# A hand-ordered list of operations for a row-wise sum of reciprocals is replaced by another list

## The chip, the cores and the metric

The kernel runs on one core of one Trainium2 chip. The metric is device time in microseconds (us), the median over several executions. One more execution was recorded by the hardware profiler; every time of an instruction comes from that one.

## The reference

```python
"x": np.abs(np.random.randn(32, 512, 1024)).astype(np.float32) + 1e-6

def reference(x):
    return np.sum(1.0 / x, axis=-1).astype(np.float32)
```

The input holds 32 x 512 = 16,384 vectors of 1024 fp32 values, 67.1 MB. The output is one sum for each vector.

## The kernel before

The vectors are laid over 128 partitions, 128 vectors for each. What the kernel calls a row r is one vector in every partition: a tile of 128 x 1024 fp32, 512 KB. The rows lie in a ring of 40 places in SBUF (`ring`, row r in place r % 40).

The kernel does not divide element by element. It splits a row into its halves a and b and uses 1/a + 1/b = (a + b) / (ab). So half as many reciprocals are needed, and these are made by ScalarE as exp(-ln(ab)), with a scale of 2^17 that is taken out again in the last step. The steps of a row are:

- **D** (line 185, SP queue): the load. `D10` loads the next ten rows with one DMA.
- **P** (line 197, POOL), or **W** (line 218, DVE), or **C** and **V**: the product ab into a slot of `prod`. C (line 207) lets PE copy the half b into a PSUM bank by a matmul with the identity, V (line 218) multiplies on DVE with that bank; W multiplies two SBUF operands on DVE.
- **L** (line 240, ACT): Ln of the product, in place.
- **E** (line 249, ACT): Exp of minus that. With a bank number (`E8+2@6`) the result goes to PSUM, without one it stays in `prod`.
- **S** (line 230, PE): a + b into a PSUM bank, by two matmuls with the identity. Only some rows have it.
- **R** (line 265, DVE): the sum over the row. A row with S multiplies the 512 reciprocals with the 512 sums in PSUM and accumulates. A row without S multiplies all 1024 elements in the ring with the reciprocals, used twice, and accumulates; that instruction has twice the columns.

The order of all this is written out by hand in the string `PLAN`. A token is the step's letter, the row, `+2` where two neighbouring rows share an instruction, and after `@` a PSUM bank or, for L, the first of 22 slots of `prod`. Each engine executes its own tokens strictly in the order of the list; POOL, ACT, DVE, PE and the SP queue run beside each other and wait for one another through semaphores that follow from who reads and writes which ring place, slot or bank. So a token that has to wait holds up everything behind it on its engine.

The last two rows, 126 and 127, are cut in two halves of columns. The pieces are numbered 126 and 127 (the first halves) and 128 and 129 (the second halves), have 256-column instructions where others have 512, and are loaded one by one (256 KB each):

```python
def place(r):
    if r < LAST:
        return r, 0, H
    part, q = divmod(r - LAST, F - LAST)
    return LAST + q, part * H, H // 2
```

Loads use a DMA each, split where the ring wraps. A place in the ring may be written again when its row's product and its S (or, without S, its R) are done, so a D token stands behind those steps of the row 40 places earlier. After the last token one DMA writes the sums (line 282).

Of the kernel before, what the change touches and what calls it, by code (L numbers as in the profile page):

```python
# [11 lines left out]
def kernel(  # L12
# [22 lines left out]


    PLAN = """
        D2 D10 D15 D13 P0+2 C3@3 S2@0 V3 P2 L0@0 L1@1 C11@3 S3@1 E0@6 E1@7 P4+2 V11 L2@3 L3@2
        R0 S6@2 E2 E3 R1 P6+2 L4+2@4 R2 R3 E4+2@6 S7@0 P8+2 L6+2@8 R4 S10@1 E6+2 R5 D7 P10
        L8+2@10 R6 R7 S11@2 E8+2@6 L10+2@6 R8 E10+2 R9 R10 R11 P12+2 C19@3 S14@0 V19 P14+2  # L40
        L12+2@12 S15@1 E12+2@6 S18@2 R12 P16+2 L14+2@16 R13 E14+2 R14 P18 L16+2@18 R15 S19@0
        E16+2@6 P20+2 L18+2@14 R16 D10 S22@1 E18+2 R17 P22+2 L20+2@20 R18 R19 E20+2@6 S23@2
        P24+2 L22+2@0 R20 S26@0 E22+2 R21 D7 P26 L24+2@2 R22 C27@3 R23 E24+2@6 P28+2 S27@1
        V27 R24 L26+2@4 C35@3 R25 E26+2 P30+2 S30@2 L28+2@8 V35 R26 E28+2@6 R27 S31@0 P32+2
        L30+2@10 R28 E30+2 S34@1 R29 D8 P34 L32+2@12 R30 R31 P36+2 E32+2@6 S35@2 L34+2@6 R32
        C43@3 E34+2 R33 P38+2 S38@0 L36+2@16 R34 R35 E36+2@6 S39@1 V43 P40+2 L38+2@18 R36
        S42@2 E38+2 R37 D8 P42 L40+2@20 R38 R39 E40+2@6 S43@0 P44+2 L42+2@14 R40 S46@1 E42+2
        R41 D4 L44+2@0 R42 R43 E44+2@6 P46+2 C51@3 R44 S47@0 V51 P48+2 L46+2@2 R45 S50@2
        E46+2 R46 P50 L48+2@8 R47 S51@1 E48+2@6 P52+2 L50+2@4 R48 S54@0 E50+2 R49 D6 P54+2
        C59@3 L52+2@10 R50 R51 E52+2@6 S55@2 V59 P56+2 L54+2@12 R52 S58@1 E54+2 R53 D6 P58  # L50
        L56+2@16 R54 R55 S59@0 E56+2@6 P60+2 L58+2@6 R56 S62@2 E58+2 R57 D4 P62+2 L60+2@18
        R58 R59 C67@3 E60+2@6 P64+2 S63@0 L62+2@20 V67 R60 E62+2 S66@1 R61 D4 P66 L64+2@14
        R62 E64+2@6 P68+2 R63 S67@2 L66+2@0 R64 E66+2 S70@0 R65 D3 P70+2 L68+2@2 R66 R67
        E68+2@6 S71@1 L70+2@8 R68 D2 P72+2 C75@3 E70+2 R69 D3 S74@2 V75 P74 L72+2@4 R70 R71
        S75@0 E72+2@6 P76+2 L74+2@10 R72 S78@1 E74+2 R73 D2 D1 P78+2 L76+2@12 C83@6 R74 R75
        E76+2@4 S79@2 V83 P81 L78+2@16 R76 D2 S81@0 L83@6 W80 E78+2 W82 E83@7 R77 D2 D1
        S80@3 D1 D1 L82@7 L80+2@18 R83 P86 S86@4 E82@6 R78 P87 L86@20 R79 E80+2 S84@1 R82 D1
        D1 P84 D1 E86 R80 P89 L84@21 S89@2 R81 E84 R86 P85 L89@0 R84 E89 W88 L85@1 R89 E85@7
        P90+2 C93@6 L87+2@14 R85 D1 C95@5 E87+2@3 V93 S92@0 V95 P94 L90+2@2 R88 L95@4 S93@1
        P92 R87 D2 D1 D1 E90+2@6 E95@5 P98 R91 S97@2 L92+2@8 P99 R90 L94@5 S96@3 E92+2 R95  # L60
        P96+2 E94@7 L98+2@10 R92 R94 E98+2@5 P101+2 S100@0 R93 L96+2@12 R98 E96+2 R99 P100
        L101+2@6 R97 L100@16 P106 C104@7 R96 E101+2@5 S105@1 V104 P105 E100 R102 L104@19
        P107 S104@2 L105+2@17 R101 E104 P108 R100 E105+2 S106@3 R104 L107+2@20 W103 R105
        L103@0 P109 C110@7 R106 E107+2@5 S111@0 V110 P111 E103@4 R107 L109@1 P113 S112@1
        L110+2@14 R108 E109@7 P114 R103 E110+2 S110@2 W112 L113+2@2 R111 L112@4 P115 S116@3
        R109 E113+2@5 R110 P116 L115@5 R114 E112 E115@7 C118@4 P117 L116@10 R112 S117@0 V118
        E116 P119 L117@11 R115 L118@8 P120 S119@1 E117 R116 E118@7 R117 P121 L119+2@12 R118
        S120@0 E119+2 P122 R113 L121@9 R119 P123 L122@6 R120 E121@7 E122@6 R121 P124 S124@0
        L123@7 E123@5 R122 P125 L124@16 S125@1 E124 R123 P127 L125@19 L127@17 W126 S126@2
        E125 W128 P129 R124 L126@18 S129@3 E127@7 R125 E126 S128@0 L129@21 R127 L128@20 E129  # L70
        R126 E128 R129 R128
    """.split()

    Ln = mybir.ActivationFunctionType.Ln
# [238 lines left out]
```

## Time and profile before

| what | value |
|---|---|
| median of 4 runs | 169.12 us (169.03 to 169.23) |
| the profiled execution | 169.04 us |
| its span, first to last instruction | 167.2 us |
| busy PE, DVE, ACT, POOL | 132.7, 128.3, 133.0, 128.0 us |
| bytes read | 67.11 MB, 402 GB/s over the span |
| loads | 32, from 7,680 KB down to 256 KB |

Busy time counts compute instructions; waits, semaphores and the issue of DMAs do not count. The profile's page cuts the span into 40 slices and gives the busy share of each in tenths. The view of stretches gives busy microseconds of each engine in a stretch of time, with the number of instructions in brackets. The chain of waits is followed back from the last instruction, at each step to what released it. In a timeline a row has the start, the time, the engine, the line, the operation with its tiles and shapes, and how many instructions were merged; what stands in square brackets is idle time before it.

### The profile page before, as it was taken

To read this page: it belongs to the slowest core of one execution; us is meant where nothing else is said; L and a number is where in the kernel's file an instruction comes from. 1 tells how busy PE (TensorE), PEld (TensorE's weight loads), DVE (VectorE), ACT (ScalarE), POOL (GpSimd) and SP (SyncE) were. 2 spreads that over 40 slices of the span, in tenths; PEclk is the share of its full clock that TensorE was granted. 3 is DMA by queue.
4 is the path that set the end of the run, shared out by engine and by line. 5 is a ranking of instruction groups with operands and counts; after the bars stand their busy time and mean duration, and the time that the engine had idled before them with its cause. 6 is when DMAs were issued, how large, how long until landed. Compare 5 with 4: busy or idle time off the path is not lost.

```text
span 167.2 us, 1334 instructions
## 1 busy us (share of the span) xinstructions
PE 132.7 (79%) x292; PEld 54.9 (33%) x292; DVE 128.3 (77%) x283; ACT 133.0 (80%) x161; POOL 128.0 (77%) x80
## 2 busy tenths in 40 slices
PE   0000799949989999977998999999699679989692
PEld 0000333214433434323333434434244134424261
DVE  0000129864789989886798898799999999999994
ACT  3040255917999999977999997999899999999992
POOL 1500795049999999939999997966899997979970
PEclk9999999987999999999999999999999999999998
DMA  5999999999999998999999999999999999999910
GB/s 186 535 392 392 470 470 470 470 408 408 408 408 407 432 472 367 451 423 412 423 463 416 439 404 449 423 437 412 419 427 424 425 427 411 418 408 411 397 63 16
DMA packets 4760, 67.26 MB, mean 402 GB/s; under 512 B 528, under 2 KB 656, under 8 KB 2192
## 3 DMA queue, kind: packets, MB, share of 16 engines
q1 hardware_dynamic: 4752, 67.18, 94.9%
q14 instruction: 6, 0.05, 0.1%
q8 instruction: 2, 0.03, 0.1%
HBM read 67.11 MB, written 0.07 MB: 402 GB/s over the span
## 4 chain that ended last, share of the span: by engine, by line
DMA 61%; POOL 14%; DVE 10%; issue 9%; ACT 3%; PE 1%; SPq 0%; DVEq 0%; POOLq 0%
DMA ring<-in_x_dram 61%; POOL prod L197 14%; DVE ring L265 6%; DVE prod L265 3%; ACT prod L240 1%; ACT ps L249 1%; DVE prod L218 1%; PE ps L207 1%; DVE sums L265 0%; SPq L185 0%; DVEq L308 0%; POOLq L197 0%
## 5 line engine op out<-in xcount | busy, mean ns | idle before, releaser
L197 POOL TENSOR_TENSOR prod<-ring 128x1024 f32<-128x1024 f32 (+2 forms) x74 | 127.3, 1754 | 33.7 <-DMA ring<-in_x_dram 31.7
L230 PE MATMUL ps<-ring,ident 128*128 128x512 f32 (+1 forms) x260 | 118.0, 601 | 5.5 <-DVE sums L265 4.2
L240 ACT ACTIVATE prod<-prod 128x1024 f32<-128x1024 f32 (+2 forms) x80 | 69.1, 876 | 24.9 <-POOL prod L197 23.2
L265 DVE CUSTOM_DVE_ANT_1 ring<-ring,ps 128x1024 f32<-128x1024 f32 (+1 forms) x65 | 76.3, 1208 | 9.0 <-ACT ps L249 9.0
L230 PEld LDWEIGHTS ps<-ring,ident 128*128 128x128 f32 x260 | 49.2, 194 | 72.9 <-issue 50.2
L265 DVE CUSTOM_DVE_ANT_0 prod<-prod,ps 128x512 f32<-128x512 f32 (+1 forms) x63 | 40.7, 678 | 1.3 <-ACT prod L249 1.3
L207 PE MATMUL ps<-ring,ident 128*128 128x512 f32 x32 | 18.3, 658 | 25.8 <-DMA ring<-in_x_dram 25.8
L249 ACT ACTIVATE ps<-prod 128x1024 f32<-128x1024 f32 (+2 forms) x40 | 33.9, 854 | 4.7 <-DVE sums L265 3.9
L249 ACT ACTIVATE prod<-prod 128x1024 f32<-128x1024 f32 (+2 forms) x40 | 34.6, 875 | 0.8
L218 DVE TENSOR_TENSOR prod<-ring,ps 128x512 f32<-128x512 f32 x16 | 10.9, 684 | 26.1 <-PE ps L207 25.8
L207 PEld LDWEIGHTS ps<-ring,ident 128*128 128x128 f32 x32 | 5.7, 201 | 35.8 <-issue 21.1
L265 DVE DVE_READ_ACCUMULATOR2_ANT sums<- 128x1 f32 x130 | 10.7, 82 | 0.0
L218 DVE TENSOR_TENSOR prod<-ring 128x512 f32<-128x512 f32 (+1 forms) x7 | 4.5, 661 | 0.0
L83 ACT ACT_TABLE_LOAD x1 | 1.3, 1283 | 0.7 <-PEq L297 0.7
L265 DVE CUSTOM_DVE_ANT_0 prod<-prod,ps,sums 128x256 f32<-128x256 f32 x2 | 0.9, 474 | 0.0
masks.py:197 POOL MEMSET ident<- 128x128 f32 x1 | 0.2, 205 | 0.3 <-POOLq L297 0.3
masks.py:199 POOL TENSOR_SCALAR_AFFINE_SELECT ident<-ident 128x128 f32<-128x128 f32 x1 | 0.3, 292 | 0.1
L297 POOL MEMSET const-float32-0.0<- 128x1 f32 x1 | 0.1, 98 | 0.2 <-issue 0.2
L297 POOL MEMSET const-bfloat16-1.0<- 128x1 bf16 x1 | 0.1, 101 | 0.0
L297 POOL MEMSET const-uint8-127<- 128x1 uint8 x1 | 0.1, 101 | 0.0
L297 POOL MEMSET const-float32-1.0<- 128x1 f32 x1 | 0.1, 98 | 0.0
## 6 DMA issues: line engine op xcount, KB each, us to landing
ring<-in_x_dram SPq DMA_DIRECT2D x2, 5120.0 KB, 21.9
ring<-in_x_dram SPq DMA_DIRECT2D x2, 4096.0 KB, 32.4
ring<-in_x_dram SPq DMA_DIRECT2D x1, 7680.0 KB, 34.2
ring<-in_x_dram SPq DMA_DIRECT2D x2, 3584.0 KB, 30.3
ring<-in_x_dram SPq DMA_DIRECT2D x1, 6656.0 KB, 49.5
ring<-in_x_dram SPq DMA_DIRECT2D x3, 2048.0 KB, 34.8
ring<-in_x_dram SPq DMA_DIRECT2D x2, 3072.0 KB, 32.5
ring<-in_x_dram SPq DMA_DIRECT2D x5, 1024.0 KB, 26.0
```

Source lines behind the costliest of these rows:

```text
L83: nc.scalar.add_instruction(mybir.InstLoadActFuncSet(name=nc.get_next_instruction_name(), act_func_set_id=act_sets.index("natural_log_exp_ ...
L197: inst = nc.gpsimd.tensor_tensor(out=prod[:, p : p + m, :w], in0=ring[:, a : a + m, at : at + w], in1=ring[:, a : a + m, at + w : at + 2 * w],
L207: inst = nc.tensor.matmul(ps[:, b, : place(r)[2]], lhsT=ident, rhs=xs(r, 1), start=True, stop=True,)
L218: inst = nc.vector.tensor_tensor(out=prod[:, p, :w], in0=xs(r, 0), in1=in1, op=mult)
L230: inst = nc.tensor.matmul(ps[:, b, : place(r)[2]], lhsT=ident, rhs=xs(r, h), start=h == 0, stop=h == 1,)
L240: inst = nc.scalar.activation(out=pg, in_=pg, func=Ln, scale=S)
L249: inst = nc.scalar.activation(out=rc, in_=pg, func=Exp, scale=-1.0)
L265: inst = nc.vector.tensor_tensor_reduce(out=row, in0=row, in1=other, scale=S, scalar=total if q in summed else 0.0, op0=mult, op1=add, acc ...
L297: nc = _bacc.Bacc("TRN2", target_bir_lowering=False, num_devices=1)
```

## The change

Only the string `PLAN` changes. The tokens for each row stay of the same kinds; their order, the sizes of the loads, the pairing of rows, the slots and banks change. Up to row 79 the same rows have P, C and V, and S as before. From row 80 on the choice which row is multiplied by which engine, and which row has an S, is another: P is done for rows 83, 82, 85, 84, 86, 91, ... instead of 81, 86, 87, 84, 89, 85, ..., and the four half-row pieces get their product from P (before: 126 and 128 from W, 127 and 129 from P).

The loads were 2, 10, 15, 13, 7, 10, 7, 8, 8, 4, 6, 6, 4, 4, 3, 2, 3, 2, 1, 2, 2 rows, then 7 single rows and 4 half-rows, 32 in all. They become 2, 10, 14, 14, 10, 10, 6, 8, 6, 6, 6, 4, 4, 3, 3, 3, 2, 2, 2 rows, then 11 single rows and 4 half-rows, 34 in all.

The new list, the old one being in the code above:

```diff
     PLAN = """
+        D2 D10 D14 D14 P0+2 C3@3 S2@0 V3 P2 L0+2@0 C11@3 S3@1 E0+2@6 P4+2 V11 L2+2@2 R0 S6@2
+        E2+2 R1 P6+2 L4+2@4 R2 R3 E4+2@6 S7@0 P8+2 L6+2@8 R4 S10@1 E6+2 R5 P10 L8+2@10 R6 R7
+        S11@2 E8+2@6 L10+2@6 R8 E10+2 R9 D10 R10 R11 P12+2 C19@3 S14@0 V19 P14+2 L12+2@12
+        S15@1 E12+2@6 S18@2 R12 P16+2 L14+2@16 R13 E14+2 R14 P18 L16+2@18 R15 S19@0 E16+2@6
+        P20+2 L18+2@14 R16 S22@1 E18+2 R17 D10 P22+2 L20+2@20 R18 R19 E20+2@6 S23@2 P24+2
+        L22+2@0 R20 E22+2 R21 L24+2@2 R22 R23 E24+2@6 P26 C27@3 R24 S26@0 P28+2 V27 R25 D6
+        L26+2@4 C35@3 E26+2 S27@1 P30+2 V35 L28+2@8 R26 S30@2 R27 E28+2@6 P32+2 L30+2@10 R28
+        S31@0 E30+2 R29 P34 L32+2@12 S34@1 R30 R31 E32+2@6 P36+2 S35@0 L34+2@6 R32 E34+2 R33
+        D8 P38+2 S38@2 L36+2@16 R34 R35 E36+2@6 C43@3 P40+2 L38+2@18 S39@0 R36 E38+2 V43
+        S42@1 R37 D6 P42 L40+2@14 R38 E40+2@6 P44+2 R39 S43@2 L42+2@20 R40 E42+2 R41 S46@0
+        P46+2 L44+2@0 R42 R43 E44+2@6 S47@1 P48+2 L46+2@2 R44 E46+2 R45 D6 L48+2@4 P50 C51@3
+        R46 R47 S50@0 E48+2@6 V51 P52+2 R48 L50+2@8 C59@3 E50+2 R49 S51@1 D6 P54+2 L52+2@10
+        V59 R50 E52+2@6 S54@2 R51 P56+2 L54+2@12 R52 S55@0 E54+2 R53 D4 P58 L56+2@16 R54
+        S58@1 R55 E56+2@6 P60+2 S59@0 L58+2@6 R56 E58+2 R57 D4 P62+2 S62@2 L60+2@14 R58 R59
+        E60+2@6 S63@1 P64+2 L62+2@18 R60 E62+2 R61 D3 L64+2@20 R62 P66 C67@3 R63 E64+2@6
+        S66@0 V67 P68+2 R64 L66+2@0 S67@1 E66+2 R65 D3 P70+2 L68+2@2 R66 S70@2 R67 E68+2@6
+        P72+2 S71@0 L70+2@4 R68 D3 E70+2 R69 D2 C75@3 P74 L72+2@10 R70 S74@1 V75 E72+2@6
+        P76+2 R71 S75@2 L74+2@8 R72 D2 E74+2 R73 D2 D1 P78+2 S78@0 L76+2@12 R74 R75 E76+2@6
+        S79@1 L78+2@16 R76 D1 P83 C81@5 E78+2 R77 D1 D1 D1 P82 S83@2 L83@6 V81 P85 E83 R78
+        L82@7 S80@3 R79 L81@14 P84 R83 E82 E81@7 W80 D1 S82@0 L85@15 R81 D1 D1 D1 L84@18
+        E85@6 E84@5 R85 P86 C88@7 L80@19 E80 R82 C87@4 P91 L86@20 R80 S91@0 E86@6 V88 P89+2
+        L91@21 V87 L88@0 R86 S88@1 E91 E88 R91 L87@3 P95 R84 D1 D1 D1 S92@2 L89+2@1 P94 R88
+        E87@7 E89+2@5 S93@0 R87 D1 D1 D1 P93 L94+2@4 R90 P92 L93@10 R89 E94+2@3 C98@7 P96
+        E93 R95 S97@1 L92@11 P99 L96@8 R94 E92 S96@4 E96 W97 L99@9 V98 L97@12 P100+2 R92
+        E99@7 S102@3 R96 E97 R99 L98@13 E98@6 P102 R97 L100+2@16 R98 P103 C105@7 L102@6
+        E100+2@4 R93 S105@1 P104 V105 E102 R101 L103@14 S103@0 L104@15 R102 E103 P106 E104@7
+        R100 C107@6 R103 P108 L105+2@18 S106@2 V107 E105+2 R104 P109+2 S109@0 L107+2@20 R106
+        R105 E107+2@6 S110@2 P111 L109+2@0 R107 P112 E109+2 R108 C114@6 P113 L111+2@2 R110
+        S113@1 R109 E111+2@4 P115 V114 L113@7 R111 P116 S116@0 L114+2@4 R112 E113 P117
+        E114+2@6 S117@2 R113 P118 L116+2@8 R115 E116+2 P119 S119@1 R114 L118@11 R117 P120
+        L119@13 R116 E118@7 E119 R118 P121 S121@0 L120@12 E120@6 R119 P122 L121@10 S122@2
+        R120 E121 P123 L122@16 R121 E122 S123@1 W124 L123@17 R122 L124@6 E123 W125 S125@0
+        E124@7 R123 P126 L125@15 R124 P127 L126@14 E125 S128@1 P128 E126@6 R125 L127@18 P129
+        S129@2 L128@19 R126 E127@7 E128 R127 L129@20 R128 E129 R129
     """.split()
```

More of the change, by code (lines that the diff above doesn't have):

```diff
@@ L37 @@
     PLAN = """
[L38 to L71, printed above, removed]
+        D2 D10 D14 D14 P0+2 C3@3 S2@0 V3 P2 L0+2@0 C11@3 S3@1 E0+2@6 P4+2 V11 L2+2@2 R0 S6@2
+        E2+2 R1 P6+2 L4+2@4 R2 R3 E4+2@6 S7@0 P8+2 L6+2@8 R4 S10@1 E6+2 R5 P10 L8+2@10 R6 R7
+        S11@2 E8+2@6 L10+2@6 R8 E10+2 R9 D10 R10 R11 P12+2 C19@3 S14@0 V19 P14+2 L12+2@12
```

## The prediction

> **What bounds the kernel now.** I read the page's slices and queues first, then the busy time by stretch, then the chain that ended last, then the last microseconds engine by engine.
>
> ```profile
> DMA  5999999999999998999999999999999999999910
> q1 hardware_dynamic: 4752, 67.18, 94.9%
> ```
>
> The loads keep the transfer engines full from the second slice to the last but two. The completion records of the loads in the trace say the same: the first two rows land at 5.75 us, each later load right behind the one before it, the last half-row at 161.37. Successive landings fit 0.075 us a load plus 1.206 us a row (fifteen rows 18.15, eight 9.72, two 2.49, one 1.28; half a row 0.64). No list of operations gets below that floor; it can only change what is late behind it.
>
> ```profile
> core 0: us, PE busy (x) PEld busy (x) DVE busy (x) ACT busy (x) POOL busy (x), PEclk, DMA share, GB/s
> 70.00:80.00 10.00, 8.15 (x19) 3.20 (x18) 7.85 (x17) 7.56 (x8) 7.37 (x5) 1.00 0.98 417
> ...
> 110.00:120.00 10.00, 9.91 (x24) 4.06 (x22) 10.00 (x24) 9.33 (x15) 7.09 (x7) 1.00 0.99 421
> ...
> 150.00:160.00 10.00, 8.51 (x20) 3.57 (x21) 9.92 (x24) 9.73 (x17) 9.87 (x8) 1.00 0.96 375
> 160.00:167.20 7.20, 4.01 (x16) 2.63 (x14) 4.72 (x16) 4.05 (x11) 1.79 (x3) 0.93 0.06 18
> ```
>
> From 110 us DVE has no hole: it works off a backlog while rows land. At 70 to 80 us all three wait for one big load.
>
> ```profile
> 126.26 23.59 DMA ring<-in_x_dram
> 149.85 0.14 issue
> 149.98 1.11 PE ps L207 x2
> 151.09 0.02 issue
> 151.12 0.69 DVE prod L218
> ```
>
> After row 118 has landed (149.85) the chain is DVE to the end: 13.6 us without a real hole.
>
> ```profile
> 162.78 0.71 ACT L240 ACTIVATE prod<-prod 128x256 f32<-128x256 f32 x2
> 163.39 0.71 ACT L249 ACTIVATE prod<-prod 128x256 f32<-128x256 f32 x2
> ...
> 163.84 0.47 DVE L265 CUSTOM_DVE_ANT_0 prod<-prod,ps,sums 128x256 f32<-128x256 f32 x1
> 164.24 0.47 DVE L265 CUSTOM_DVE_ANT_0 prod<-prod,ps,sums 128x256 f32<-128x256 f32 x1
> ```
>
> The last half-row's reduction starts 2.9 us after its landing and ends, with its accumulator read, at 164.72; 2.45 us of output transfer follow to the span's 167.17. So two things can be won: up to about 1 us between landing and last reduction, and no more, since product (0.8), Ln (0.4), Exp (0.4) and reduction (0.5) must follow the landing: 161.4 + 0.15 + 2.1 = 163.7.
>
> **The change, part by part.** Durations, start to start where an engine is full: POOL product 1.28 one row, 2.35 two; ACT 1.04 two rows (0.95 behind an independent one), 0.52 one row (0.65 behind its own Ln), 0.31 half a row; DVE reduction 1.14 with 1024 columns, 0.61 with 512 (a row summed by PE), DVE product 0.61; PE sum 1.72, copy 0.86.
>
> *Loads.* 34 instead of 32. The counts are equal at rows 95, 99, 108 and 114 (12, 13, 16 and 19 loads), so these land as before: 121.30, 126.19, 137.25, 144.71. Behind them 11 single rows and 4 halves stand for 2 doubles, 7 singles and 4 halves: 2 x 0.075 = +0.15. Last landing 161.5. A rule speaks against this: the Trainium skill, "DMA: Bandwidth & Descriptors", section "Bandwidth", wants batches of 1 MiB or more, and its section "Anatomy of one DMA" puts about 2 us of fixed time on each. By that, two more loads cost 4 us. But in this queue a single (512 KB) lands 1.27 to 1.29 after its forerunner and a double 2.49 to 2.52 after it: 0.02 to 0.08 a load, since the next one runs behind it. I take the row. Every load needs its ring row free and the completion of an older load (the SP queue waited 15 times for a landing). The ring is free long before: single rows 117 to 119 are listed after R77 (done at 111), the last after R87 (124). So it is the completions that pace the singles, as before, where the last of them were still issued 7.7 us ahead of landing. No gap in the queue.
>
> *Rows 12 to 80.* 14 and 14 instead of 15 and 13: row 26 comes with the second, at 51.6, so POOL starts rows 28 on 0.5 us later and ACT at row 40 0.3 later. Rows 40 to 49 land at 64.4 and POOL needs them at 65.8: no wait. Rows 50 to 59 land at 77.3, POOL is there at 76.4: 0.9 us idle where before it idled 2.63 for row 47. With 66 to 73 at 94.4, POOL ends rows 72+73 at 102.7 (before 104.13) and 76+77 at 106.4 (107.70). Ln of row 76 moves from 108.25 to 106.9, R76 on DVE from 110.41 to 109.0: 1.4 us earlier. The eight single Ln and Exp of rows 0 to 3 become four double ones: worth nothing, since ACT waits for data there (3.9 us at 27).
>
> *Work from row 80 on.* DVE before: 24 reductions of 1.14, 22 of 0.61, 11 products of 0.61, halves 0.61 + 3 x 0.4 + 2 x 0.38: 50.1 us. After: 23 of 1.14, 23 of 0.61, 11 products, halves 2 x 0.61 + 2 x 0.4: 49.0. Minus 1.1. POOL takes four half-rows instead of two: +1.6, in a stretch where it has room. ACT has 9 pairs of rows instead of 12, so three Ln and three Exp more: a row costs 0.52 alone and 0.48 to 0.52 in a pair, and at most 0.13 more behind its own Ln, +0.3 in all. PE has one sum more, one half sum less and one copy more, +1.7, in a stretch where it is busy 8.5 of 10 us and ahead of DVE.
>
> *The queues in the new order.* Working the list down by these durations: R76 starts 109.0, R83 ends 113.7, then W80. Row and rule weighed again:
>
> ```profile
> 119.11 1.29 POOL L197 TENSOR_TENSOR prod<-ring 128x512 f32<-128x512 f32 x1
> ...
> 119.90 1.04 DVE L218 TENSOR_TENSOR prod<-ring 128x512 f32<-128x512 f32 x1
> ```
>
> W88 took 1.04 beside a POOL product, others 0.69: +0.35. The Trainium skill ("SBUF — State Buffer", section "Who interferes with whom") has the later of the two fully blocked: for W80, met in the middle of P84, up to 0.6. I take 0.5 (W88 ended 0.55 after POOL's end, near a full block), and R85's wait for its Exp (0.45) absorbs it. W97 and W124 meet an idle POOL. Further on DVE waits for Exp 0.25 at R87, 0.2 at R95, 0.7 at R107, 0.3 at R115, and ends R121 at 157.5. ACT runs without a hole to L118 (152.1) and then follows the landings. Row 124 lands at 157.65; W124, in front of R122, starts at 157.75. The wait costs 0.25 and hides nothing late. Then L124 at 158.45, and ACT is the chain: four full intervals to L126 (160.53), L126 0.31, E125 0.52, E126, L127, L128, E127, E128 0.31 each, L129 at 162.9, E129 at 163.3, done 163.75. R129 163.78 to 164.26. POOL has finished the last half-row at 162.65, so it isn't late.
>
> **Sum.** Last reduction 164.26 against 164.72: -0.46. The profiled execution took 169.04 (span 167.2 and 1.84 around it), so 168.58; the runs shown have their median 0.08 above it: 168.7.
>
> **The rivals.**
> *Holes in the queues eat it (same).* For it: DVE reaches W124 only 0.25 before its data, and every duration above ignores handover times of 0.03 to 0.1. If 0.3 to 0.8 us gather, the end stands at 164.5 to 165.0: 168.9 to 169.4.
> *Head of line at W124 (slower).* DVE works in order: if it comes to W124 after 158.2 (0.5 late beyond the data), L124 and the whole ACT tail move with it. My list has 2.3 us of DVE holes between 109 and 157; before had about 1.5 with a longer backlog. If single-row alternation in the list (E99@7 behind V98, L97 behind W97, L119 in front of E118) makes 1.2 to 2 us more, it ends 165.2 to 166.0: 169.6 to 170.4. Against: 1.4 us head start and 1.1 us less work are on DVE's side.
> *The full gain.* No wait at W124 or in ACT: end at 163.8: 168.2.
> That it doesn't do what it says: the two SP queues do have the loads named, so no chance.
>
> **How the numbers follow.** A measurement here can tell about 0.2% (0.34 us). Forecast with the full gain: 0.52, under 168.78. Holes: 0.28. Head of line: 0.20. Range: the floor 163.7 gives 168.1, the inner half of the slower case reaches 170.0; its outer part and gains by another placement of stalls on single transfer engines stay outside.
>
> **What would show it.** Right: last landing near 161.5; POOL's wait of 2.6 us at 71 to 74 replaced by one near 1 at 76; R76 near 109; DVE idle just before W124; four half-row products on POOL; last reduction ending 164.0 to 164.5. Wrong: a landing later than 162; DVE without a hole from 150 to the end; ACT waiting for W97, V98 or W124 by more than 0.5.

## The result, and the profile after

| what | before | after |
|---|---|---|
| median | 169.04 us (168.83 to 169.54, 51 runs) | 168.62 us (168.35 to 169.18, 32 runs) |
| ratio after / before | | 0.9977 (95% interval 0.9972 to 0.9982) |
| profiled execution, its span | 169.04, 167.2 us | 168.48, 166.6 us |
| last landing in the profiled execution | 161.37 us | 161.22 us |
| last reduction, accumulator read | 164.72 us | 164.03 us |
| busy PE, DVE, ACT, POOL | 132.7, 128.3, 133.0, 128.0 us | 133.4, 128.1, 133.4, 129.5 us |

The kernel became 0.23% faster, about 0.4 us; the forecast was 168.7. In late_part (2 of 8), in dve_plus (5 of 22) and once in before, executions took 2.4 to 4.2 us longer than the rest; the ratios leave these out.

The page after, its slices of the transfer engines and its first queue:

```profile
DMA  5998999999999899989999999999999999999920
q1 hardware_dynamic: 5040, 67.18, 95.2%
```

The transfer engines are as full as before, so the change worked behind the landings or not at all. The same stretches as before (start and end, length, busy time of each engine with its instructions in brackets, granted clock, DMA share, GB/s):

```profile
core 0: us, PE busy (x) PEld busy (x) DVE busy (x) ACT busy (x) POOL busy (x), PEclk, DMA share, GB/s
70.00:80.00 10.00, 9.58 (x22) 3.83 (x21) 9.51 (x24) 9.48 (x10) 9.24 (x5) 1.00 1.00 428
110.00:120.00 10.00, 9.46 (x23) 3.99 (x22) 9.94 (x21) 9.50 (x17) 7.46 (x7) 1.00 1.00 422
120.00:130.00 10.00, 9.05 (x22) 3.83 (x21) 9.68 (x20) 9.94 (x17) 8.87 (x8) 1.00 1.00 423
130.00:140.00 10.00, 8.88 (x21) 3.72 (x20) 9.98 (x24) 9.09 (x15) 8.75 (x7) 1.00 1.00 419
140.00:150.00 10.00, 9.33 (x23) 3.86 (x22) 9.31 (x22) 9.86 (x12) 9.88 (x8) 1.00 1.02 412
150.00:160.00 10.00, 9.24 (x22) 3.75 (x21) 9.65 (x23) 9.87 (x17) 7.94 (x7) 1.00 0.96 375
160.00:166.60 6.60, 2.71 (x10) 1.44 (x8) 3.96 (x14) 3.48 (x10) 2.33 (x4) 0.86 0.06 20
```

The hole at 70 to 80 us is mostly gone on POOL, ACT and DVE (DVE 9.51 instead of 7.85). Late on DVE shows holes, 0.69 us of them at 140 to 150 and 0.35 at 150 to 160, where before it had 0.08 in the last of these stretches. So DVE no longer carries a backlog into the last 10 us. The chain that ended last, of after, in its last microseconds (start, time, what):

```profile
149.92 1.06 ACT prod L240
...
157.69 1.11 ACT prod L240 x2
158.80 0.52 ACT prod L249
159.32 0.49 ACT ps L249
159.81 0.90 ACT prod L240 x2
160.71 0.53 ACT prod L249
161.24 0.02 issue
161.26 0.69 DVE prod L265
...
163.57 0.45 DVE prod L265
```

Before it was DVE for 13.6 us. Now ACT holds it from 149.92 until 161.24, and DVE only for the reductions that follow. How ACT meets the landing of row 124 is seen in DVE's timeline of after:

```profile
156.54 0.69 DVE L265 CUSTOM_DVE_ANT_0 prod<-prod,ps 128x512 f32<-128x512 f32 x1
...
157.44 0.69 DVE L218 TENSOR_TENSOR prod<-ring 128x512 f32<-128x512 f32 x1 [0.21 <-DMA ring<-in_x_dram]
...
163.55 0.48 DVE L265 CUSTOM_DVE_ANT_0 prod<-prod,ps,sums 128x256 f32<-128x256 f32 x1
```

DVE has ended R121, waits 0.21 us for row 124 (landed 157.42) and starts W124 at once. W124 ends at 158.13 and its Ln, L124, starts at 158.17. That is 0.57 us behind the start of the Ln ahead of it, where one that waits for nothing follows in 0.52. So ACT is full and meets row 124 almost as it comes: later data would hold it up, earlier data would win it 0.05 us. The last row of the fence is R129; before, the last reduction (R128 in that order) started at 164.24.

### The profile page after: what moved, and what is told of

Read it like the earlier page. It is cut to its first block, busy times and chain, and to the rows that moved or that the text cites. A ratio compares the mean times of both kernels' runs of the same rounds, so it can differ in the third digit from the quotient of the medians.

```text
span 166.6 us, 1350 instructions
## 1 busy us (share of the span) xinstructions
PE 133.4 (80%) x294; PEld 56.2 (34%) x294; DVE 128.1 (77%) x281; ACT 133.4 (80%) x163; POOL 129.5 (78%) x82
## 4 chain that ended last, share of the span: by engine, by line
DMA 48%; POOL 19%; ACT 11%; DVE 11%; issue 8%; SPq 0%; POOLq 0%; DVEq 0%
DMA ring<-in_x_dram 48%; POOL prod L197 19%; DVE ring L265 6%; ACT prod L240 6%; ACT prod L249 3%; DVE prod L265 3%; ACT ps L249 2%; DVE prod L218 1%; DVE sums L265 0%; SPq L185 0%; POOLq L197 0%; DVEq L308 0%
## 5 line engine op out<-in xcount | busy, mean ns | idle before, releaser
L197 POOL TENSOR_TENSOR prod<-ring 128x1024 f32<-128x1024 f32 (+2 forms) x76 | 128.8, 1729 | 32.2 <-DMA ring<-in_x_dram 29.9
L230 PEld LDWEIGHTS ps<-ring,ident 128*128 128x128 f32 x260 | 50.3, 196 | 68.1 <-issue 54.8
L207 PE MATMUL ps<-ring,ident 128*128 128x512 f32 x34 | 20.1, 680 | 27.4 <-DMA ring<-in_x_dram 27.4
L265 DVE CUSTOM_DVE_ANT_0 prod<-prod,ps 128x512 f32<-128x512 f32 x63 | 41.4, 683 | 0.8 <-PE ps L230 0.4
L218 DVE TENSOR_TENSOR prod<-ring,ps 128x512 f32<-128x512 f32 x17 | 11.5, 684 | 26.0 <-PE ps L207 26.0
L207 PEld LDWEIGHTS ps<-ring,ident 128*128 128x128 f32 x34 | 5.9, 196 | 37.9 <-issue 22.7
L218 DVE TENSOR_TENSOR prod<-ring 128x512 f32<-128x512 f32 x4 | 3.0, 754 | 0.2 <-DMA ring<-in_x_dram 0.2
```

The lines of the kernel that those rows point to most:

```text
L197: inst = nc.gpsimd.tensor_tensor(out=prod[:, p : p + m, :w], in0=ring[:, a : a + m, at : at + w], in1=ring[:, a : a + m, at + w : at + 2 * w],
L207: inst = nc.tensor.matmul(ps[:, b, : place(r)[2]], lhsT=ident, rhs=xs(r, 1), start=True, stop=True,)
L218: inst = nc.vector.tensor_tensor(out=prod[:, p, :w], in0=xs(r, 0), in1=in1, op=mult)
L230: inst = nc.tensor.matmul(ps[:, b, : place(r)[2]], lhsT=ident, rhs=xs(r, h), start=h == 0, stop=h == 1,)
L265: inst = nc.vector.tensor_tensor_reduce(out=row, in0=row, in1=other, scale=S, scalar=total if q in summed else 0.0, op0=mult, op1=add, acc ...
```

## The experiments

In the expectations, T1 is the prediction's account (DVE gets its backlog off through the head start and the smaller work, and the last products stand so that the end follows the landing); T2 gives the gain to the times at which the late rows land; T3 gives it to the other assignment of the last products alone. Every ratio is against before, measured beside the kernel (its median was 168.98 to 169.04 each time).

**Which half of the list.** Row 80 starts a load in both lists, so they can be joined there. First the old list and its loads up to row 79, and the new ones from row 80 on. The PSUM banks of the S steps behind the join, and of E76, are renumbered so that the two parts don't meet in one. (In the first two edits minus is the new list; `...` stands for tokens left out.)

```diff
-    D2 D10 D14 D14 ... D10 ... D10 ... D6 ... D8 ... D6
+    D2 D10 D15 D13 ... D7 ... D10 ... D7 ... D8 ... D8
```

> The old list and the old loads for rows 0 to 79, the new list and the new loads from row 80 on. Theory 1 (the new list ends where ACT's work behind W124 ends, and DVE is there in time through an earlier R76 and 1.1 us less work): R76 near 110.4 instead of 108.75, the holes of DVE between 119 and 145 take up most of the 1.6, DVE reaches W124 0 to 0.4 late: 168.6 to 169.0. Theory 2 (only the landings count): last landing and time as in the new list, 168.6. Theory 3 (only the products of the half-rows count, which left DVE): 168.6.

Measured: 168.55 us, ratio 0.9973 (0.9962 to 0.9984). The whole gain of the median is there without a change of order or loads ahead of row 80. What the head start is still good for is seen below, at W97. Then the other half: the new list up to row 79, the old one from row 80 on.

```diff
-    ... D6 ... D6 ... D4 ... D4 ... D3 ... P83 C81@5
+    ... D4 ... D6 ... D6 ... D4 ... D4 ... C83@6
```

> The new list and loads for rows 0 to 79, the old list and the old loads from row 80 on. Theory 1: DVE's unbroken run to the end starts some 1.6 us earlier and does the old work, so it meets its data again near the end: last reduction 164.2 to 164.6, 168.5 to 168.9. Theories 2 and 3: the late loads and the late products are the old ones, so 169.0.

Measured: 169.14 us, ratio 1.0002 (0.9994 to 1.001), no difference. Where the head start goes is in the waits of early_part at 100 to 120 us (engine and what it waited for: us in total, times, longest), first fence, and of before at 105 to 120, second fence:

```profile
POOL prod L196 <- DMA ring<-in_x_dram: 4.3, 1, 4.3
```

```profile
POOL prod L197 <- DMA ring<-in_x_dram: 2.9, 1, 2.9
```

POOL comes 1.4 us earlier and waits 1.4 us longer, for one load: rows 84 to 89 of the old list, which land together at 114.04 in before and 114.05 here. (The line numbers of this kernel are one lower.) The timelines show the wait pass on to ACT and DVE. Early_part:

```profile
114.19 6.21 POOL L196 TENSOR_TENSOR prod<-ring 128x512 f32<-128x512 f32 x5 [4.34 <-DMA ring<-in_x_dram]
117.97 0.63 ACT L239 ACTIVATE prod<-prod 128x512 f32<-128x512 f32 x1 [0.37 <-POOL prod L196]
119.30 0.69 DVE L264 CUSTOM_DVE_ANT_0 prod<-prod,ps 128x512 f32<-128x512 f32 x1 [0.28 <-ACT prod L248]
```

Before:

```profile
117.96 0.63 ACT L240 ACTIVATE prod<-prod 128x512 f32<-128x512 f32 x1 [0.38 <-POOL prod L197]
119.29 0.69 DVE L265 CUSTOM_DVE_ANT_0 prod<-prod,ps 128x512 f32<-128x512 f32 x1
```

Ln of row 84 starts at 117.97 and 117.96, its reduction at 119.30 and 119.29. The old list sets its clock anew there, and nothing gained before can pass. In the new list row 84 comes with rows 80 to 85 at 108.71. So T1 as the prediction had it (the head start carries the gain) is wrong for the median, and the gain sits behind row 80.

**Is it DVE's smaller work?** The new list asks about 1.1 us less of DVE. Two products, of rows 88 and 87, are done twice, which gives about that back.

```diff
-    V88 P89+2 L91@21 V87
+    V88 V88 P89+2 L91@21 V87 V87
```

> The new list with V88 and V87 done twice in a row (the second time the same result): 1.2 us more work on DVE at 118 to 120 us, so that DVE has the old list's amount. Theory A (the 1.1 us less work on DVE is not the gain; the holes behind, some 1.4 us with 0.2 in front of W124, take it up): 168.6 to 168.8. Theory B (DVE's amount of work sets the end): 169.5 to 169.8.

Measured: 168.59 us, ratio 0.998 (0.9966 to 0.9994): nothing lost in the median. Its stretches:

```profile
120.00:130.00 10.00, 9.03 (x22) 3.81 (x21) 10.00 (x20) 9.52 (x16) 8.84 (x8) 1.00 1.00 424
130.00:140.00 10.00, 8.87 (x21) 3.72 (x20) 10.00 (x24) 9.47 (x16) 9.10 (x7) 1.00 1.01 420
140.00:150.00 10.00, 9.47 (x22) 3.76 (x21) 9.96 (x23) 9.87 (x12) 9.88 (x8) 1.00 1.01 409
150.00:160.00 10.00, 9.24 (x22) 3.75 (x21) 9.66 (x23) 9.87 (x17) 7.94 (x7) 1.00 0.97 379
```

From 120 to 150 us DVE has 0.04 us of holes instead of 1.03 (0.32 + 0.02 + 0.69) in after: 0.99 of the added 1.2 us went into waits. DVE's waits between 109 and 157.3, of after and then of dve_plus, name them:

```profile
DVE ring L265 <- ACT ps L249: 1.1, 2, 0.6
DVE prod L265 <- ACT prod L249: 0.3, 1, 0.3
```

```profile
DVE ring L265 <- ACT ps L249: 0.5, 1, 0.5
```

The 0.5 that stays is R76's wait, which ends at 108.7 and so lies ahead of the two doubled products. In the last 10 us before 160 the two are alike (9.65 and 9.66). The time that DVE had won it spent waiting for Exp, so 1.1 us of it could be given back.

**The last products.** Five kernels move them, three in the new list and two in the old. Half-rows 126 and 128 from POOL to DVE, as the old list had it:

```diff
-    P126 ... P128
+    W126 ... W128
```

> The new list with the products of the half-rows 126 and 128 on DVE (W126, W128 in place of P126, P128). Theory 1: DVE is full from W125 to the end, so 2 x 0.38 us of products move its end by 0.4 to 0.8: 169.0 to 169.4. Theory 2: 168.6. Theory 3: the whole gain is gone, 169.0.

Measured: 169.11 us, ratio 1.0012 (1.0002 to 1.0022). DVE's timeline:

```profile
160.29 0.42 DVE L218 TENSOR_TENSOR prod<-ring 128x256 f32<-128x256 f32 x1
...
161.76 0.42 DVE L218 TENSOR_TENSOR prod<-ring 128x256 f32<-128x256 f32 x1
...
164.33 0.48 DVE L265 CUSTOM_DVE_ANT_0 prod<-prod,ps,sums 128x256 f32<-128x256 f32 x1
```

The two products take 0.34 us each (start to start), and R129 starts 0.78 later than after's 163.55. Row 124 was late in this execution (W124 started at 157.77); counted from the start of W124, R129 is 0.46 later, about as much as the medians differ (0.49). Next, W124 one place back:

```diff
-    W124 L123@17 R122 L124@6
+    L123@17 R122 W124 L124@6
```

> The new list with W124 behind R122 instead of in front of it. Theory 1: W124 starts at 158.3 instead of 157.4, L124 0.8 later, and ACT has no slack behind it: +0.5 to +0.8, 169.1 to 169.4. A wait in front of R122 that costs (head of line) would make this one faster: 168.4. Theories 2 and 3: 168.6.

Measured: 169.36 us, ratio 1.0026 (1.0014 to 1.0038). The product starts at 158.21 instead of 157.44, and ACT waits for it:

```profile
158.93 0.63 ACT L240 ACTIVATE prod<-prod 128x512 f32<-128x512 f32 x1 [0.85 <-DVE prod L218]
```

The 0.2 us that DVE idles in front of row 124 buys 0.7: R122 can wait, ACT can't. Next, products 124 and 125 on POOL, as the old list had them:

```diff
-    W124 ... W125
+    P124 ... P125
```

> The new list with the products of rows 124 and 125 on POOL instead of DVE. Theory 1: POOL gets 2 x 1.28 us in front of the four half-rows, P124 is done at 158.8 where W124 was at 158.1, and P129 at 163.0 instead of 162.3: +0.3 to +0.7, 168.9 to 169.3. If DVE's amount of work is what sets the end, 1.2 us less of it gives up to 0.4 off: 168.2 to 168.6.

Measured: 169.26 us, ratio 1.0017 (1.0009 to 1.0025). ACT's timeline:

```profile
158.85 0.63 ACT L240 ACTIVATE prod<-prod 128x512 f32<-128x512 f32 x1 [0.65 <-POOL prod L197]
```

A POOL product of a row takes about 1.3 us where DVE takes 0.7, and on the path from landing to Ln that difference is the loss. Last, half-rows 126 and 128 to POOL in the old list:

```diff
-    W126 ... W128
+    P126 ... P128
```

> The old list with all four half-row products on POOL (P126, P128 in place of W126, W128). Theory 1: DVE loses 0.76 us of work, but POOL, which has rows 124 and 125 as well, ends the last half-row at 163.2 instead of 162.35, so nothing is won: 169.0 to 169.4. Theory 3: this alone is the gain: 168.6.

Measured: 169.29 us, ratio 1.0015 (1.0009 to 1.0022), slower than before. ACT's timeline:

```profile
162.88 0.72 ACT L240 ACTIVATE prod<-prod 128x256 f32<-128x256 f32 x2 [0.22 <-POOL prod L197]
```

There POOL still has products 124 and 125 ahead of four halves. So the halves alone are no gain. With both moves in the old list:

```diff
-    P124 ... P125 ... W126 ... W128
+    W124 ... W125 ... P126 ... P128
```

> The old list with the new assignment of the last products: rows 124 and 125 on DVE, all four half-rows on POOL. Theory A (the assignment of the last products is the gain by itself): 168.6. Theory B (it pays only where DVE has room for two full products more; the old list's DVE is full to its end): DVE gets 2 x 0.61 and loses 2 x 0.38, +0.4 to +0.5, 169.3 to 169.6.

Measured: 170.12 us, ratio 1.0064 (1.0052 to 1.0076), slower than before by 1.1 us and beyond what was expected. Its timelines of DVE, then of POOL:

```profile
160.48 1.10 DVE L218 TENSOR_TENSOR prod<-ring 128x512 f32<-128x512 f32 x1
160.31 3.25 POOL L197 TENSOR_TENSOR prod<-ring 128x256 f32<-128x256 f32 x4 [2.67 <-DMA ring<-in_x_dram]
```

DVE comes to W125 at 160.48, 1.7 us after its landing (158.82 in before), and meets the first of POOL's four half-rows: 1.10 us instead of 0.69. T3 falls with this. The new assignment is good only behind a list in which DVE has worked its backlog off by row 124.

**Do the new operations need the new late loads?** The new operations with the new loads to row 79, but the old load sizes from there:

```diff
-    ... D6 ... D6 ... D4 ... D4 ... D3 ... D3 ... D3
+    ... D4 ... D6 ... D6 ... D4 ... D4 ... D3 ... D2
```

> The new list with the old load sizes from row 80 on (4, 6, 6, 4, 4, 3, 2, 3, 2, 1, 2, 2 rows, then singles, instead of 6, 6, 4, 4, 3, 3, 3, 2, 2, 2 and singles). If the sizes of the loads only had to fit somehow: 168.6. If the order is cut to its landings: rows 84 and 85 land at 114.05 instead of 108.7 and rows 90 and 91 at 121.3 instead of 116.3, where P85 and P91 want them at 111.3 and 117.6; ACT stands 3 to 5 us and has 1.2 us of holes behind: 170.5 to 172.

Measured: 173.3 us, ratio 1.0247 (1.0226 to 1.0268), worse than expected. Waits at 105 to 125 us:

```profile
POOL prod L196 <- DMA ring<-in_x_dram: 6.8, 2, 3.6
...
ACT prod L239 <- POOL prod L196: 4.1, 3, 1.8
...
DVE ring L264 <- ACT ps L248: 3.4, 2, 2.9
```

The last landing is 161.30, much as in after, and yet the end is 4.7 us later (168.74 instead of 164.03). The time of the last landing alone decides nothing; what matters is which rows are there when each engine comes to them, so this order needs these load sizes. That the late landings are the cause by themselves (T2) is refuted by the three moves above: tail_w, w124_late and p124_p125 keep every late load of the new list and lose the whole gain. The reverse of this run, the old operations with the new late loads, was not tried.

**The price of a load.** The 34 loads of the new list without any compute (products, Ln, Exp and sums are all left out; one element of each of the ring places of the last 12 rows and half-rows is copied out, to wait for them):

```diff
-    D2 D10 D14 D14 P0+2 C3@3 S2@0 V3 ... R129
+    D2 D10 D14 D14 D10 D10 D6 D8 D6 ... D1 D1 D1
```

> The 34 loads of the new list alone, no product, no logarithm, no reduction (the sums are left out; one element of the last rows is read to wait for them). If the landings are set by the transfer engines and by nothing that the compute engines do, the last lands at 161.2 as in the new list. If the six transfers of program code that lie in the stream (8 and 16 KB, 3.3 us together) hold up the engines that carry them, it lands 1 to 1.6 us earlier, and first and last completion of a load lie closer together than the 1.9 us seen.

Measured: 164.67 us, ratio 0.9742 (0.9729 to 0.9755), last landing 160.03. And the same with every row loaded by itself, 130 loads:

```diff
-    D2 D10 D14 D14 D10 D10 D6 D8 D6 ... D1 D1 D1
+    D1 D1 D1 ... D1
```

> The same rows with no compute, each in a load of its own, 130 loads instead of 34. With 0.075 us a load (the slope of the landings): 96 x 0.075 = 7.2 us more than loads alone. With a fixed 2 us for each load that nothing hides: 190 us more. With nothing but the packets' own sizes: 0 to 4.

Measured: 173.32 us, ratio 1.0244 (1.0212 to 1.0276). The pages of loads_only, then of loads_singles (packets, MB, share of the 16 engines):

```profile
q1 hardware_dynamic: 5040, 67.18, 97.4%
```

```profile
q1 hardware_dynamic: 18864, 67.18, 98.9%
```

96 more loads cost 8.65 us, 0.090 us each, with the engines busy throughout: the price lies within the transfers and is no pause between them. Two loads more are then 0.18 us; the 2 us of the rule that the prediction weighed would have made the 96 loads 190 us longer.

**The margin at W97.** In after W97 starts at 128.96 and ends just before POOL's double product P100 starts at 129.87. Here it is moved into it:

```diff
-    W97 L99@9 V98 L97@12 P100+2 R92 E99@7
+    L99@9 V98 P100+2 R92 W97 L97@12 E99@7
```

> The new list with W97 (and L97) behind V98 and R92, so that W97 is met by DVE 0.3 us after P100+2 has started on POOL. If the two only slow each other a little: W97 0.7 to 1.05 us as beside P85, 168.6 to 169.4. If a DVE product with both inputs in SBUF is blocked for all of POOL's instruction: W97 takes 2.5 to 2.8 us, L97 and Exp behind it come 3 us later and not all of it is made good: 170.0 to 171.5.

Measured: 170.78 us, ratio 1.0101 (1.0078 to 1.0124). Timelines of POOL (P100 with what follows it, merged), then of DVE:

```profile
130.10 4.02 POOL L197 TENSOR_TENSOR prod<-ring 128x1024 f32<-128x1024 f32 x2 [1.09 <-DMA ring<-in_x_dram]
130.39 2.60 DVE L218 TENSOR_TENSOR prod<-ring 128x512 f32<-128x512 f32 x1
```

The product of one row takes 2.60 us instead of 0.69. P100 itself runs from 130.10 to 132.44, so DVE has stood until POOL was through and then needed another 0.55. A place 1.4 us later in a queue costs 2.2 us in all.

The same meeting is seen in kernels that leave W97 in its place. In dve_plus DVE comes to it 0.81 us later than in after, 0.17 ahead of P100, and the product takes its usual time:

```profile
129.76 0.69 DVE L218 TENSOR_TENSOR prod<-ring 128x512 f32<-128x512 f32 x1
129.93 3.99 POOL L197 TENSOR_TENSOR prod<-ring 128x1024 f32<-128x1024 f32 x2 [1.12 <-DVE sums L265]
```

In late_part, which has no head start, DVE comes to it 1.20 later. In the profiled execution, which took 172.68 us, that was 0.05 behind P100:

```profile
130.16 2.85 DVE L218 TENSOR_TENSOR prod<-ring 128x512 f32<-128x512 f32 x1
130.11 4.03 POOL L197 TENSOR_TENSOR prod<-ring 128x1024 f32<-128x1024 f32 x2 [1.10 <-DMA ring<-in_x_dram]
```

DVE is 1.2 us behind after's times up to W97, 3.4 from the next instruction on and 4.3 at the end. In after W97 starts 0.92 ahead of P100, and the longest of its 32 executions took 169.18 us. So the head start and the lighter work buy something that the medians do not show: distance from this meeting. That the other six long executions of late_part and dve_plus met it too is likely, but there is no trace of them, so it is not shown.

## Why the prediction was right, and where its steps were not

*The floor.* Right: the engines stay full and the last landing is near 161.5 (161.22). The term "2 x 0.075 = +0.15" came out as -0.15. The price of a load was 0.090 rather than 0.075, so the sign is not from there; single executions of these kernels have their last landing anywhere from 161.1 to 161.9, and 0.15 can't be read from one of each. The step asked more of two profiles than they can give. (One double of before, rows 115 and 116, landed 2.63 us after its forerunner, outside the quoted 2.49 to 2.52.) The weighing of row against rule, however, holds: the row's small price is the one that was measured.

*Rows 12 to 80.* Right in every number: POOL waits 0.76 at 77.21 (forecast 0.9 from 76.4), ends rows 72+73 at 102.50 (102.7) and 76+77 at 106.07 (106.4), R76 starts at 108.75 (109.0):

```profile
77.21 3.61 POOL L197 TENSOR_TENSOR prod<-ring 128x512 f32<-128x512 f32 x2 [0.76 <-DMA ring<-in_x_dram]
```

But early_part and late_part show that the 1.4 us head start does not move the median by itself. The prediction put it "on DVE's side" and had not looked at what a late list does with it: the load of rows 84 to 89 stops it in the old list, and the new list does not need it.

*Work from row 80 on.* The sums by engine came out: POOL +1.5 (forecast +1.6), ACT +0.4 (+0.3), PE +0.7 (forecast +1.7, too much, without effect). DVE's instructions changed in number as counted, and from start to start they took what they were priced at (1.14, 0.61). Its busy time fell by 0.2 only; that view counts the overlap of two instructions that follow each other once (64 reductions of 1217 ns before are 77.9 us and are booked as 75.7), and what lies between 0.2 and 1.1 was not traced further. It doesn't decide: dve_plus shows that the 1.1 are not needed. So both of DVE's advantages, each 1.1 to 1.4 us, are reserves: with either of them gone the median stays, but a quarter of the executions of these two kernels took 2.5 to 4.2 us longer. What happens with both gone at once wasn't tried.

*The queues.* W80 in the middle of P84 was booked with +0.5:

```profile
113.46 0.94 DVE L218 TENSOR_TENSOR prod<-ring 128x512 f32<-128x512 f32 x1
```

It took 0.94, so 0.25 more than alone and not 0.5, and was through 0.55 after POOL, as taken from W88. "W97 and W124 meet an idle POOL" held, for W97 with 0.92 us from start to start, a margin that the working did not see: 2 us and more stand behind it (w97_in_p100, late_part). W124 started 0.08 before POOL's last full row ended, without harm. DVE's losses came out in sum but not in place. From R76's start to R121's end it took 48.47 us, 2.2 more than its 55 instructions at the prediction's prices (46.3); the list had 2.3, and before, counted the same way, 1.5. But only the wait at R107 came as listed (0.63 for 0.7). Those at R85, R87, R95 and R115 were 0.06 or less, and 0.27 at R91 was not in the list. That the sum fits is luck. (The sentence that DVE has no hole from 110 us in before is too strong: it idles 0.7 us in all from 109 to 157.) From there on the tail is close: R121 ended at 157.23 (157.5), W124 started at 157.44 (157.75), L124 at 158.17 (158.45), L129 at 162.66 (162.9), E129 at 163.10 (163.3), R129 ended at 164.03 (164.26). The whole tail runs 0.2 to 0.3 early, the landing of row 124 (157.42 for 157.65) included: from that landing to the end of the last reduction it is 6.61 us, as worked out. POOL had the last half-row done at 162.33 (162.65), not late.

*The sum.* Forecast -0.46 at the last reduction; the two profiled executions differ by 0.69 there, the medians by 0.42.

*The rivals.* Holes did gather, as many as the list had, and did no harm, since they lie ahead of row 124. Head of line at W124 did not come: DVE was 0.21 early for it. The full gain (end at 163.8) was missed by 0.2.

What carried the gain of the median, then: DVE reaches row 124 as it lands, its product goes ahead of older reductions, POOL takes the short halves. Each of these is needed (tail_w, w124_late and p124_p125 lose 0.5 to 0.7 us against after). They are not sufficient by themselves (before_new_tail), and the order from row 80 on with the loads cut to it makes the rest (late_part, new_ops_old_late_loads). Which single row of that order makes DVE come to row 124 in time stays open. No experiment pointed to a version that beats both kernels.

## What to carry to other kernels

When an engine is made earlier or lighter, look for the next landing that everything hangs on: time won ahead of it is lost there, and only work behind it counts. But look at the longest executions too before you call a reserve worthless: it may be what keeps two instructions apart that must not meet. At the end of a stream that is bound by transfers, give the product of the newest row to the faster engine and put it in front of older work, even if the engine idles a little for it. An order written by hand and the sizes of its loads are one design: half of it was worth nothing, or cost 4 us.

## What the runs showed of the hardware

A DVE product of two SBUF operands that starts beside a POOL product stands until that one ends: 0.69 us became 2.60 beside a double row (w97_in_p100), 2.85 in late_part, 1.10 beside a half-row (before_new_tail) and 0.94 beside a row (W80). Each of them ended 0.55 us after POOL's instruction. The one that starts first is not held up: 0.69 in dve_plus. The Trainium skill, "SBUF — State Buffer", section "Who interferes with whom", says that the SBUF ports which DVE shares with GpSimd (POOL) are an exclusive lock, which whoever issues first holds for its whole instruction, and these rows agree. That 0.2 us decide between nothing and 2 us (dve_plus 0.17 ahead of POOL, late_part 0.05 behind it) was not expected.

The transfers have a floor of their own, 164.67 us without compute, 4 us below the kernel; 1.2 us of this lie in the landings (160.03 instead of 161.22 in after) and not in what is behind them. In loads_only the first and the last of the 16 transfer engines finish a load 0.3 to 0.6 us apart, in after 1.7 to 2.1 from row 50 on. The trace of after has transfers of instruction code within the stream, of which loads_only has none; but loads_singles shows the same 2.0 from its fourth row on, and the one such transfer on its page comes only at 97 us, so that can't be the only cause. It stays open.
